# Six of the eight output-projection columns by seven-product blocks in a fused decoder layer

## The chip, the cores and the metric

The kernel runs on one NeuronCore of a Trainium2 chip. The metric is the device time of one execution in microseconds (us). Three timed runs of the kernel before gave 1549.17, 1547.85 and 1546.90 us; their median is 1547.85 us. Engines are named TensorE (PE; its weight loads are PEld), VectorE (DVE), ScalarE (ACT), GpSimd (POOL) and SyncE (SP, which issues most transfers).

## The reference

One layer of a decoder trunk, batch 1, 512 tokens, width 1024, all in float32:

```python
h = x + 0.5 * swiglu(rmsnorm(h, ffn1_norm), ffn1_w_in, ffn1_w_out)
h = h + hybrid_mixer(rmsnorm(h, mix_norm), ...)
h = h + 0.5 * swiglu(rmsnorm(h, ffn2_norm), ffn2_w_in, ffn2_w_out)
return rmsnorm(h, final_norm)

# the end of hybrid_mixer: two branches, merged by gates, then the output projection
y = sigmoid(gate_h) * y_h + sigmoid(gate_g) * y_g      # 512 x 1024
return y @ w_out                                       # w_out is 1024 x 1024
```

The change is in this last product `y @ w_out`, in what surrounds it (the merge ahead, the residual and the norm behind) and in the first steps of the second feed-forward block (FFN2).

## The kernel before

Activations lie transposed: a column tile is 128 features (partitions) by 512 tokens, so the width of 1024 is eight column tiles. A float32 product is made of three matmuls (`mm3`, lines 199 to 202): each operand is split into a high part, rounded by ScalarE, and a low part, the rest, subtracted by VectorE; high by high, high by low and low by high are summed in PSUM. So every slab of weights (128 x 512) costs a load, a ScalarE cast and a VectorE subtraction before TensorE can use it. The split weights lie in a ring of six buffers (`pair`, `WB = 6`), so a slab can be split once TensorE has finished the one six before it.

**Output projection** (lines 2250 to 2255). For each of eight columns d: the residual `hr` is loaded from `hd` in DRAM, `dense` does 8 blocks of 128 features with two slabs of four (24 matmuls of 512 tokens), VectorE adds half the sum to the residual (`h[:, d]`, line 2254), and `nextnorm` prepares FFN2: `prep` (line 224) writes `uh[:, d]` by ScalarE and `ul[:, d]` by VectorE, `sqacc` (line 230) squares the column on ScalarE and adds it to `acc`; here the add is GpSimd's, but for the first column (none) and the last (VectorE, line 697). The operands `ms[k]` come from `merged(k)` (lines 1900 to 1934): after the branch product of column k is complete, VectorE joins the gated branches, ScalarE and VectorE split the result.

**FFN2** (`ffn`, line 477; `stream`, line 292) runs units of four feature blocks in a fixed order: units 0 to 11 are plain (12 matmuls of 512 tokens, three pairs of columns p = 0, 1, 2), and from unit 12 on each pair is made of seven products of half the tokens (12 matmuls of 256; `seven`, `four`, `fast`): a 2 x 2 block of weights times a 2 x 2 block of activations by seven multiplications in place of eight, with sums of operands before and of results behind. `operands` (line 456) makes the activations' combinations. The norm of FFN2 comes late: units 0 to 3 run on values that are not divided by the root of the mean square yet. `stats` gives two steps, `sums` (eight narrow matmuls on `acc`, then VectorE and GpSimd for the root) and `spread` (the roots to all partitions, copied to `rbc` by ScalarE); they are hooked ahead of units 1 and 2 (line 530), and everything that needs `rbc` starts at unit 3 (`start = 3`).

**What sets the order.** The mixer up to `D.run()` and all of FFN2 have an order written out by the program (inside `manual_schedule`); for the mixer a planner (`Desk`) with costs per instruction and ranks hands out the engines' turns. The output projection between them is ordered by the framework's scheduler, which fills each engine's queue by its own estimate of when things are ready; the slab splits are marked `high_priority`. On the chip each queue then runs strictly in that order.

Of the kernel before, what the change touches and what calls it, by code (L numbers as in the profile page):

```python
# [29 lines left out]
C_F1, C_MX, C_F2, C_FN, C_HN, C_GN, C_LB, C_CV = 0, 8, 16, 24, 32, 33, 34, 50  # L30
# [15 lines left out]
TA = 6  # L46
# [102 lines left out]
def body(tc, xT, cst, sqc, hmask, dta, w1o, w1a, w2a, wt, wn, wab, wbh, wbg, wo, w1b, w2b, gfin, y, dbg=None):  # L149
# [91 lines left out]
    def stats(pl, *parts):  # L241

        def sums():
            pt = psc.tile([P, T], F32, tag="pd", name="pst")
            for i in range(NT):
                for n, x in enumerate(parts):
                    pe.matmul(pt[:, i:i + 1], x[:, i * P:(i + 1) * P], ones[:, :1], start=n == 0, stop=n == len(parts) - 1)
            root(pl, pt[:, :4], rcol)

        def spread():  # L250
            pb = psc.tile([P, T], F32, tag="pd", name="pbc")
            for i in range(NT):
# [224 lines left out]
    def ffn(w1, w2, c0, after, slow, lead=None, last=None):  # L477

        with tc.tile_pool(name="ff", bufs=1) as fp, \
# [40 lines left out]
            if lead is not None:  # L520
                pts, rest = opening(fp)
                lead()
                hooks[0] = [rest]
                for p in range(2):
                    f = columns([lambda x=x: x for x in pts[2 * p:2 * p + 2]], p, p == 1)
                    for t, x in zip((0, 0, 0, 1), f):
                        hooks.setdefault(t, []).append(x)
                done, start = 2, 1
            else:
                hooks[1], hooks[2] = ([f] for f in stats(fp, acc))  # L530
                start = 3
            for p in range(done, slow):
                us = []
                for n in range(2):
                    x, held = plain(w1[ORDER[p], n], KD, ux, lane("a" if lead is None else "b") if p == done and (lead is None or n == 0) else mm, fold=FOLD1[lead is None][p], roomy=lambda k: n if lead is not None or p else 0)
                    units += x
                    us.append((len(units) - 1, held))
                f = columns([lambda x=x: x["pt"] for _, x in us], p)
                on(max(us[0][0], start), f[0])
                on(us[1][0], f[1])  # L540
                on(us[1][0], f[2])
                hooks.setdefault(us[1][0] + 1, []).append(f[3])
            xo = operands(c0, xs, rooms, start, hooks)
            for p in range(slow, KF):
                units += fast(w1, p, xo, fp, len(units), posts, gate, late)
# [423 lines left out]
def mixer(tc, mp, e):  # L969
# [8 lines left out]
    def ps(name, lane="d"):  # L978
        return psc.tile([P, T], F32, tag="p" + lane, name=name, bufs=LANES[lane])
# [914 lines left out]
    def one(tag):  # L1894
# [2 lines left out]
            return ab[:, 0], ab[:, 1]  # L1897
        return make

    def merged(d):  # L1900

        yield "on", ("K", 7) if d < 2 else "projected", ("y", d), ("t", d), ("t", 8 + d), *([("ms", d - 3)] if d > 2 else [])
        yield "get", "mi", 1
        mi, tg = places["kn"]("mi"), places["vb"]("mt")
        yield S
        sp.dma_start(mi, md[d])
        yield S
        sp.dma_start(tg, td[d])
        g = stay.get(8 + d)
        if g is None:  # L1910
            yield "get", "ta", 1
            g = ta("mg")
            yield S
            sp.dma_start(g, td[8 + d])
        yield "lag", LAG["back"]
        yield V(512)
        dve.scalar_tensor_tensor(mi, tg, 1.0, mi, op0=ALU.add, op1=ALU.mult)
        yield "on", ("wbg", d)
        yield *V(512), 1
        dve.scalar_tensor_tensor(g, g, 1.0, pts[d], op0=ALU.add, op1=ALU.mult)  # L1920
        D.put("a" if d in (2, 3) else "mm")
        yield V(512)
        dve.tensor_tensor(g, g, mi, op=ALU.add)
        D.put("mi")
        if dbg is not None and "m" in dbg:
            sp.dma_start(dbg["m"][:, d], g)
        yield A(512)
        ab = op[d]("m", (P, 2, T), F32R)
        a, b = ms[d] = ab[:, 0], ab[:, 1]
        act.copy(a, g)  # L1930
        yield V(512)
        dve.tensor_tensor(b, g, a.bitcast(F32), op=ALU.subtract)
        D.put("ta")
        D.fire(("ms", d))

    def closing():

# [17 lines left out]

    o_h = [None] * HH
    so, ms, pts = [None] * VH, [None] * 8, {}
    stay = dict.fromkeys(STAY)
    wbgs = [(d, q) for q in range(3) for d in (0, 1)] + [(d, q) for d in (2, 3) for q in range(3)] + [(d, 3) for d in range(4)] + \
        [(d, q) for d in range(4, 8) for q in range(4)]  # L1960
    G = {"kq": [hv[:, i].rearrange("p (c a b) -> p c a b", c=NT, a=2) for i in range(3)]}
# [285 lines left out]
            sp.dma_start(dbg["og"][:, i], od[i])  # L2247


    for d in range(8):  # L2250
        hr = ta("hr")
        sp.dma_start(hr, hd[d])
        pt = dense(wo[d], KD, lambda k: ms[k])
        dve.scalar_tensor_tensor(h[:, d], pt, 0.5, hr, op0=ALU.mult, op1=ALU.add)
        e["nextnorm"](C_F2, tag="ta", bufs=TA)(d, mp)

# [80 lines left out]
```

## Time and profile before

| what | value |
|---|---|
| median of three runs | 1547.85 us |
| profiled execution, its own time | 1547.87 us |
| its span, first to last instruction | 1546.1 us |
| PE busy | 99% of the span |
| VectorE / ScalarE / GpSimd busy | 76% / 57% / 26% |
| share of PE in the chain that ended last | 96% |
| granted TensorE clock | 0.999 of full speed |

The span is read from the profile's first line; 1.8 us of the execution's time lie outside it. A busy PE says only that matmuls follow one another: whether one kind of matmul is cheaper than another is read from the distance of their starts. Idle time of an engine that is not the bottleneck costs nothing, but an average share hides stages in which another engine is nearly full, so busy times are read stage by stage.

### The profile page before, as it was taken

What the parts mean: (1) busy time and instruction counts of PE and PEld (TensorE: products, weight loads), DVE (VectorE), ACT (ScalarE), POOL (GpSimd) and SP (SyncE); (2) the same over time, 40 slices, a digit from 0 to 9 for tenths busy, and PEclk for the clock granted to TensorE, in tenths of its full rate; (3) what the DMA queues carried; (4) which work ended last, traced back from release to release, by engine and by line L of the source; (5) the groups of instructions that cost most, each with busy time, mean ns of one, the idle gap of its engine ahead of it and who ended that gap; (6) DMA issues with size and microseconds to landing.
All of it is one profiled execution on the core that took longest, in us unless ns stands there. A gap on an engine that the chain in (4) does not pass through costs nothing.

```text
span 1546.1 us, 29433 instructions
## 1 busy us (share of the span) xinstructions
PE 1535.9 (99%) x10660; PEld 1340.0 (87%) x10660; DVE 1179.7 (76%) x2257; ACT 887.9 (57%) x1965; POOL 409.0 (26%) x727
## 2 busy tenths in 40 slices
PE   9999999999999999999999999999999999999998
PEld 8899998988888888888888878888888899999897
DVE  6988887678786778678888887865554799988765
ACT  5766776454454345556676676555423576676543
POOL 0211221110221212536534655450001221121000
PEclk9999999999999999999999999999999999999999
DMA  5866866543213223654463675566554587786751
GB/s 190 190 167 171 190 163 150 154 120 109 84 45 94 65 81 117 191 181 147 134 208 119 190 224 164 171 191 187 153 192 130 157 185 194 194 194 172 192 123 64
DMA packets 159538, 237.57 MB, mean 154 GB/s; under 512 B 23312, under 2 KB 54672, under 8 KB 159392
## 3 DMA queue, kind: packets, MB, share of 16 engines
q1 hardware_dynamic: 138944, 199.63, 41.5%
q0 software_dynamic: 17568, 31.47, 12.7%
q10 hardware_dynamic: 2880, 4.59, 1.0%
q8 instruction: 84, 1.38, 0.4%
q14 instruction: 62, 0.51, 0.1%
HBM read 206.50 MB, written 29.13 MB: 152 GB/s over the span
## 4 chain that ended last, share of the span: by engine, by line
PE 96%; DMA 1%; ACT 1%; DVE 1%; issue 0%; SPq 0%; POOLq 0%; POOL 0%; ACTq 0%; DVEq 0%
PE pmm L200 17%; PE pmm L202 17%; PE pmm L201 17%; PE px L202 8%; PE px L200 8%; PE px L201 8%; PE pnat L200 4%; PE pnat L202 4%; PE pnat L201 4%; DMA kt<-kn 1%; PE pog L1738 1%; PE pgq L1530 1%; PE pw L1722 1%; PE pl L1277 1%; PE pd L1220 1%; PE pog L1736 1%
## 5 line engine op out<-in xcount | busy, mean ns | idle before, releaser
L200 PE MATMUL pmm<-uh,wp 128*128 128x512 f32 x863 | 355.2, 412 | 0.5 <-ACT ci L1397 0.3
L202 PE MATMUL pmm<-uh,wp 128*128 128x512 f32 x863 | 337.5, 391 | 0.0
L201 PE MATMUL pmm<-ul,wp 128*128 128x512 f32 x863 | 336.9, 390 | 0.0
L202 PE MATMUL px<-xs,wp 128*128 128x256 f32 x900 | 248.4, 276 | 0.0
L200 PE MATMUL px<-xs,wp 128*128 128x256 f32 x900 | 248.4, 276 | 0.0
L201 PE MATMUL px<-xs,wp 128*128 128x256 f32 x900 | 248.4, 276 | 0.0
L2103 DVE TENSOR_TENSOR wp<-raw,wp 128x512 fp32r<-128x512 f32 x226 | 159.3, 711 | 86.7 <-ACT wp L2101 83.5
L2101 ACT CAST wp<-raw 128x512 fp32r<-128x512 f32 x226 | 139.3, 619 | 137.0 <-PE pmm L202 106.5
L202 PEld LDWEIGHTS pmm<-uh,wp 128*128 128x128 f32 x863 | 162.0, 188 | 35.4
L200 PEld LDWEIGHTS pmm<-uh,wp 128*128 128x128 f32 x863 | 162.3, 188 | 33.2 <-ACT ci L1397 0.7
L201 PEld LDWEIGHTS pmm<-ul,wp 128*128 128x128 f32 x863 | 162.5, 188 | 29.7 <-DVE ul L1802 0.4
L200 PEld LDWEIGHTS px<-xs,wp 128*128 128x128 f32 x900 | 169.0, 188 | 0.1
L201 PEld LDWEIGHTS px<-xs,wp 128*128 128x128 f32 x900 | 168.9, 188 | 0.1
L202 PEld LDWEIGHTS px<-xs,wp 128*128 128x128 f32 x900 | 168.9, 188 | 0.0
L344 ACT CAST wp<-sw 128x512 fp32r<-128x512 f32 x176 | 107.9, 614 | 69.0 <-PE px L202 20.9
L319 DVE TENSOR_TENSOR wp<-sw,wp 128x512 fp32r<-128x512 f32 x176 | 120.8, 686 | 32.6 <-ACT wp L344 32.5
L344 ACT CAST wp<-rw 128x512 fp32r<-128x512 f32 (+1 forms) x132 | 80.7, 613 | 29.1 <-PE pnat L202 10.5
L1581 POOL TENSOR_TENSOR fm<-gfs,gln 128x60 f32<-128x60 f32 (+24 forms) x155 | 61.7, 398 | 92.8 <-DMA od<-zo 26.6
L1407 DVE SCALAR_TENSOR_TENSOR cy<-ci,cs,cy 128x512 f32<-128x512 f32 x96 | 72.2, 753 | 1.4
L1582 POOL TENSOR_TENSOR gln<-gln,fm 128x60 f32<-128x60 f32 (+24 forms) x155 | 64.4, 415 | 12.1
L349 POOL DMA_DIRECT2D wp<-w1b x40 | 34.7, 866 | 112.0 <-ACT wp L348 56.1
L378 DVE TENSOR_TENSOR sw<-rw 128x512 f32<-128x512 f32 x88 | 60.4, 686 | 1.7 <-DMA rw<-w2a 1.7
(587 smaller groups left out, 3496.4 us busy)
## 6 DMA issues: line engine op xcount, KB each, us to landing
raw<-wt SPq DMA_DIRECT2D x160, 256.0 KB
rw<-w1b SPq DMA_DIRECT2D x80, 256.0 KB
rw<-w1a SPq DMA_DIRECT2D x74, 256.0 KB
wp<-w1b POOLq DMA_DIRECT2D x40, 256.0 KB, 5.4
wp<-w1a POOLq DMA_DIRECT2D x35, 256.0 KB, 5.3
rw<-w2b SPq DMA_DIRECT2D x34, 256.0 KB
raw<-wn SPq DMA_DIRECT2D x32, 256.0 KB
raw<-wbg SPq DMA_DIRECT2D x32, 256.0 KB
```

The source lines that it names most:

```text
L200: pe.matmul(pt, ah, bh, start=first, stop=False)
L201: pe.matmul(pt, ah, bl, start=False, stop=False)
L202: pe.matmul(pt, al, bh, start=False, stop=last)
L319: dve.tensor_tensor(lo, x, hi.bitcast(F32), op=ALU.subtract)
L344: act.copy(hi, x)
L349: pool.dma_start(lo, units[i].fold, accum_op=ALU.add)
L378: dve.tensor_tensor(v[n], a, b, op=op)
L1407: dve.scalar_tensor_tensor(y, ci[:, j:j + T], wc[j], y, op0=ALU.mult, op1=ALU.add)
L1581: pool.tensor_tensor(tv, bc(m[:, j + 1:, j], w), t[:, j:j + 1, :w].to_broadcast([P, n, w]), op=ALU.mult)
L1582: pool.tensor_tensor(t[:, j + 1:, :w], t[:, j + 1:, :w], tv, op=ALU.add)
L2101: act.copy(hi, raw)
L2103: dve.tensor_tensor(lo, raw, hi.bitcast(F32), op=ALU.subtract)
```

## The change

Columns 0 and 1 stay as they were. Columns 2 and 3, 4 and 5, 6 and 7 are computed in pairs by `sevens(j)`, j = 1, 2, 3: seven products of 12 matmuls of 256 tokens each. `pieces(j)`, j = 0 to 3, makes the activations' combinations from the merged columns j and 4 + j, in place in `h` (where `merged` now leaves its result), and splits them; j = 0 to 2 run inside `merged(4)` to `merged(6)`, j = 3 ahead of the output projection. The residual of columns 2 to 5 is added by a transfer from `hd` that accumulates into `h`, issued by GpSimd; columns 6 and 7 load it as before and VectorE adds it. The squares of columns 1 to 6 are added to `acc` by VectorE. In FFN2 `sums`, `spread` and what needs `rbc` move back by one unit. `merged` also gives back its `ta` buffer earlier. The diff, cut where it repeats names:

```diff
+OUT = 0, 1, (2, 3), (4, 5), (6, 7)
...
-                hooks[1], hooks[2] = ([f] for f in stats(fp, acc))
-                start = 3
+                hooks[2], hooks[3] = ([f] for f in stats(fp, acc))
+                start = 4
...
-                on(us[1][0], f[1])
-                on(us[1][0], f[2])
-                hooks.setdefault(us[1][0] + 1, []).append(f[3])
+                t = max(us[1][0], start)
+                on(t, f[1])
+                on(t, f[2])
+                hooks.setdefault(t + 1, []).append(f[3])
...
+    def pieces(j):
+        x, y, lo, hi = h[:, j], h[:, 4 + j], slice(0, 256), slice(256, 512)
...
+        crossed[j] = homes[:2], homes[2:]
+        less = lambda o, a, b: (V(256), lambda: dve.tensor_tensor(o, a, b, op=ALU.subtract))
+        yield less(x[:, lo], x[:, hi], x[:, lo])
+        yield less(x[:, hi], y[:, hi], x[:, hi])
+        yield less(y[:, hi], y[:, hi], x[:, lo])
+        yield less(y[:, lo], y[:, lo], y[:, hi])
+        for z, (a, b) in zip((x, y), crossed[j]):
+            yield A(512), lambda z=z, a=a: act.copy(a, z)
+            yield V(512), lambda z=z, a=a, b=b: dve.tensor_tensor(b, z, a.bitcast(F32), op=ALU.subtract)
+
+    def sevens(j):
...
+        a11, a21, a22, a12 = (fetch(*x) for x in ((0, 0), (1, 0), (1, 1), (0, 1)))
+        bank = [ps("px", x) for x in "abde"]
+        where = {3: (0, lo), 5: (0, hi), 6: (1, lo), 0: (2, lo), 2: (2, hi), 1: (3, lo), 4: (3, hi)}
...
+        def comb(x, y, f):
+            z = places["kn"]("ws")
+            with tc.high_priority():
+                dve.tensor_tensor(z, x, y, op=f)
+            return z
+
+        def product(o, x):
+            wl, wh = e["pair"](off=SHIFT)
+            with tc.high_priority():
+                act.copy(wh, x)
+                dve.tensor_tensor(wl, x, wh.bitcast(F32), op=ALU.subtract)
+            b, c = where[o]
+            for i in range(4):
+                k, (m, t) = slice(i * P, i * P + P), moving[o](i)
+                mm3(bank[b][:, c], wh[:, k], wl[:, k], m[0][:, t], m[1][:, t], i == 0, i == 3)
+        product(0, a11)
+        s1 = comb(a21, a22, ALU.add)
+        s2 = comb(s1, a11, ALU.subtract)
+        product(2, s2)
...
+        act.mul(w[:, :256], bank[2][:, lo], 0.5)
+        dve.scalar_tensor_tensor(u, bank[2][:, hi], 0.5, w[:, :256], op0=ALU.mult, op1=ALU.add)
+        product(3, a12)
+        product(1, s1)
+        product(4, comb(a11, a21, ALU.subtract))
...
+        dve.scalar_tensor_tensor(uu, b4, 0.5, u4.to_broadcast([P, 2, 256]), op0=ALU.mult, op1=ALU.add)
+        dve.scalar_tensor_tensor(w[:, 768:], bank[3][:, lo], 0.5, w[:, 512:768], op0=ALU.mult, op1=ALU.add)
+        if j == 3:
+            for n in range(2):
+                hr = ta("hr")
+                sp.dma_start(hr, hd[2 * j + n])
+                x = w[:, n * T:n * T + T]
+                dve.tensor_tensor(x, hr, x, op=ALU.add)
+        product(6, a22)
+        product(5, comb(a12, s2, ALU.subtract))
+        act.copy(h[:, 2 * j + 1, hi], w[:, 768:])
+        for n, c in ((1, lo), (0, slice(0, T))):
+            dve.scalar_tensor_tensor(h[:, 2 * j + n, c], bank[n][:, c], 0.5, w[:, n * T:n * T + c.stop], op0=ALU.mult, op1=ALU.add)
+            if j < 3:
+                pool.dma_start(h[:, 2 * j + n], hd[2 * j + n], accum_op=ALU.add)
+        return 2 * j, 2 * j + 1
...
+        if 4 <= d < 7:
+            for need, f in pieces(d - 4):
+                yield need
+                f()
...
-    for d in range(8):
+    for need, f in pieces(3):
+        f()
+    after = e["nextnorm"](C_F2, tag="ta", bufs=TA, add=dve)
+    for step in OUT:
+        if isinstance(step, tuple):
+            for d in sevens(step[0] // 2):
+                after(d, mp)
+            continue
         hr = ta("hr")
-        sp.dma_start(hr, hd[d])
-        pt = dense(wo[d], KD, lambda k: ms[k])
-        dve.scalar_tensor_tensor(h[:, d], pt, 0.5, hr, op0=ALU.mult, op1=ALU.add)
-        e["nextnorm"](C_F2, tag="ta", bufs=TA)(d, mp)
+        sp.dma_start(hr, hd[step])
+        pt = dense(wo[step], KD, lambda k: ms[k])
+        dve.scalar_tensor_tensor(h[:, step], pt, 0.5, hr, op0=ALU.mult, op1=ALU.add)
+        after(step, mp)
```

## Rows read from the trace of the kernel before

**Rows 1.** The page's head: busy us, share of the span, instructions of each engine.
```profile
span 1546.1 us, 29433 instructions
PE 1535.9 (99%) x10660; PEld 1340.0 (87%) x10660; DVE 1179.7 (76%) x2257; ACT 887.9 (57%) x1965; POOL 409.0 (26%) x727
```

**Rows 2.** Stages: end of merge, output projection, FFN2's plain units, its seven-product units.
```profile
core 0: us, PE busy (x) PEld busy (x) DVE busy (x) ACT busy (x) POOL busy (x), PEclk, DMA share, GB/s
1144.50:1165.38 20.88, 20.88 (x94) 17.27 (x93) 8.83 (x14) 5.60 (x9) 0.00 (x0) 1.00 0.30 93
1165.38:1208.90 43.52, 43.52 (x194) 36.05 (x193) 21.78 (x32) 18.28 (x30) 7.87 (x6) 1.00 0.41 128
...
1217.20:1243.64 26.44, 26.44 (x119) 21.86 (x118) 24.77 (x31) 18.56 (x27) 6.09 (x7) 1.00 0.75 171
1243.64:1291.20 47.56, 47.56 (x421) 47.56 (x420) 44.27 (x71) 34.11 (x63) 11.23 (x13) 1.00 0.83 200
```

**Rows 3.** TensorE's timeline: start us, us, what (idle before, releaser).
```profile
1165.38 0.39 PE L200 MATMUL pmm<-m,wp 128*128 128x512 f32 x1
...
1208.90 0.39 PE L200 MATMUL pmm<-uh,wp 128*128 128x512 f32 x1
...
1246.37 0.28 PE L200 MATMUL px<-xs,ws 128*128 128x256 f32 x1
...
1247.73 0.28 PE L200 MATMUL px<-xs,wp 128*128 128x256 f32 x1
...
1251.81 0.28 PE L200 MATMUL px<-xs,wp 128*128 128x256 f32 x1
```

**Rows 4.** Weight loads by line in 1243.64:1291.20: busy us, mean ns, idle before.
```profile
L201 PEld LDWEIGHTS px<-xs,wp 128*128 128x128 f32 x124 | 23.3, 188 | 0.0
```

**Rows 5.** VectorE's timeline in FFN2 where it hardly rests.
```profile
1260.17 0.69 DVE L436 TENSOR_TENSOR luu<-px,lv 128x512 f32<-128x512 f32 x1 [0.34 <-PE px L202]
1260.90 0.42 DVE L437 TENSOR_TENSOR lv<-px,luu 128x256 f32<-128x256 f32 x1
1261.24 0.69 DVE L319 TENSOR_TENSOR wp<-sw,wp 128x512 fp32r<-128x512 f32 x1
1261.84 0.69 DVE L378 TENSOR_TENSOR sw<-rw 128x512 f32<-128x512 f32 x1
```

**Rows 6.** VectorE's timeline around the first columns of the output projection.
```profile
1163.56 0.69 DVE L196 TENSOR_TENSOR wp<-raw,wp 128x512 fp32r<-128x512 f32 x1 [2.03 <-ACT wp L195]
1165.58 0.69 DVE L1920 SCALAR_TENSOR_TENSOR tg<-tg,pmm 128x512 f32<-128x512 f32 x1 [1.33 <-PE pmm L202]
1168.26 0.69 DVE L1932 TENSOR_TENSOR m<-tg,m 128x512 fp32r<-128x512 f32 x1 [0.69 <-ACT m L1930]
1175.77 0.75 DVE L227 SCALAR_TENSOR_TENSOR ul<-h,cs,uh 128x512 fp32r<-128x512 f32 x1
1176.46 0.69 DVE L2254 SCALAR_TENSOR_TENSOR h<-pmm,hr 128x512 f32<-128x512 f32 x1
```

**Rows 7.** Transfers by issuing line, from the page: KB each, median us to landing.
```profile
wp<-w1b POOLq DMA_DIRECT2D x40, 256.0 KB, 5.4
```

**Rows 8.** ScalarE's timeline at the end of the output projection.
```profile
1210.72 0.71 ACT L226 ACTIVATE uh<-h,cs 128x512 fp32r<-128x512 f32 x1
```

**Rows 9.** VectorE's timeline from the projection's end into FFN2, and its next idle times.
```profile
1209.10 0.69 DVE L2254 SCALAR_TENSOR_TENSOR h<-pmm,hr 128x512 f32<-128x512 f32 x1 [2.67 <-PE pmm L202]
...
1211.61 0.75 DVE L227 SCALAR_TENSOR_TENSOR ul<-h,cs,uh 128x512 fp32r<-128x512 f32 x1
...
1217.22 2.74 DVE L467 SCALAR_TENSOR_TENSOR rooma<-h,cs,rbc 128x512 f32<-128x512 f32 x4
...
1222.08 0.69 DVE L516 TENSOR_TENSOR lv<-pmm,rbc 128x512 f32<-128x512 f32 x1 [1.51 <-PE pmm L202]
...
1248.61 0.68 DVE L319 TENSOR_TENSOR wp<-sw,wp 128x512 fp32r<-128x512 f32 x1
1250.65 0.69 DVE L436 TENSOR_TENSOR luu<-px,lv 128x512 f32<-128x512 f32 x1 [1.36 <-PE px L202]
```

More of the change, by code (lines that the diff above doesn't have):

```diff
@@ L1898, in one @@
         return make
+    def pieces(j):
+        x, y, lo, hi = h[:, j], h[:, 4 + j], slice(0, 256), slice(256, 512)
+        if j == 0:
+            homes = [t[:, i] for t in (places["gz"]("wz", (P, 2, T), F32R) for _ in range(2)) for i in range(2)]
+        elif j < 3:
+            homes = [places[n]("wq", dt=F32R) for n in (("on", "on", "qm", "ln"), ("gb", "gb", "at", "at"))[j - 1]]
+        else:
+            homes = [z[:, 6 + i] for i in range(2) for z in (uh, ul)]
+        crossed[j] = homes[:2], homes[2:]
[7 more added lines that the diff above has]
+            yield V(512), lambda z=z, a=a, b=b: dve.tensor_tensor(b, z, a.bitcast(F32), op=ALU.subtract)
@@ new lines, in sevens, with fetch @@
+    def sevens(j):
+        def fetch(n, q):
+            r = places["vb"]("wr")
+            sp.dma_start(r, wo[2 * j + n][:, q * T:q * T + T])
+            return r
+        lo, hi = slice(0, 256), slice(256, 512)
+        moving = {0: lambda i: (ms[i], lo), 3: lambda i: (ms[4 + i], lo), 5: lambda i: (ms[4 + i], hi),
+                  1: lambda i: (crossed[i][0], lo), 4: lambda i: (crossed[i][0], hi),
+                  6: lambda i: (crossed[i][1], lo), 2: lambda i: (crossed[i][1], hi)}
+        a11, a21, a22, a12 = (fetch(*x) for x in ((0, 0), (1, 0), (1, 1), (0, 1)))
[19 more added lines that the diff above has]
+        product(2, s2)
+        w = places["n2"]("wv", (P, 4 * 256))
+        u = places["x"]("wu", (P, 256))
+        act.mul(w[:, :256], bank[2][:, lo], 0.5)
[3 more added lines that the diff above has]
+        product(4, comb(a11, a21, ALU.subtract))
+        uu, b4, u4 = (y.rearrange("p (a t) -> p a t", t=256) for y in (w[:, 256:768], bank[3], u))
+        dve.scalar_tensor_tensor(uu, b4, 0.5, u4.to_broadcast([P, 2, 256]), op0=ALU.mult, op1=ALU.add)
[14 more added lines that the diff above has]
+        return 2 * j, 2 * j + 1
@@ L1919, in merged @@
         yield *V(512), 1
-        dve.scalar_tensor_tensor(g, g, 1.0, pts[d], op0=ALU.add, op1=ALU.mult)
+        gt = g
+        dve.scalar_tensor_tensor(gt, gt, 1.0, pts[d], op0=ALU.add, op1=ALU.mult)
         D.put("a" if d in (2, 3) else "mm")
         yield V(512)
-        dve.tensor_tensor(g, g, mi, op=ALU.add)
+        g = h[:, d]
+        dve.tensor_tensor(g, gt, mi, op=ALU.add)
         D.put("mi")
+        D.put("ta")
         if dbg is not None and "m" in dbg:
@@ L1932, in merged @@
         dve.tensor_tensor(b, g, a.bitcast(F32), op=ALU.subtract)
-        D.put("ta")
         D.fire(("ms", d))
+        if 4 <= d < 7:
+            for need, f in pieces(d - 4):
+                yield need
+                f()
     def closing():
@@ L1957, in mixer @@
     so, ms, pts = [None] * VH, [None] * 8, {}
-    stay = dict.fromkeys(STAY)
+    stay, crossed = dict.fromkeys(STAY), {}
     wbgs = [(d, q) for q in range(3) for d in (0, 1)] + [(d, q) for d in (2, 3) for q in range(3)] + [(d, 3) for d in range(4)] + \
```

## The prediction

> **What bounds the kernel now.** I read the page's head first: TensorE is busy for 99% of the span, VectorE for 76% [rows 1]. An average hides stages, so the second view is busy time by stage [rows 2]: TensorE has no hole in any of them; VectorE works half of the output projection's time (21.78 of 43.52 us), but 24.77 of 26.44 us in FFN2's plain units and 44.27 of 47.56 us in its seven-product units. The reader is to see two things there: the projection is paced by TensorE alone, and VectorE is nearly as full in the stage right behind. The third view is TensorE's timeline, since a busy matmul says nothing of its price. The projection's 192 matmuls of 512 tokens start at 1165.38 and FFN2's first at 1208.90, so 43.52 / 192 = 0.2267 us each; one product of 12 matmuls of 256 tokens goes from 1246.37 to 1247.73, so 0.1133 us each [rows 3]. Half the tokens cost exactly half the time.
>
> **What TensorE saves.** Removed: 6 columns x 24 x 0.2267 = 32.64 us. Added: 3 pairs x 7 products x 12 x 0.1133 = 28.56 us. The saving is an eighth, **4.08 us**; the projection would take 39.44 us (10.88 for columns 0 and 1, 9.52 per pair). No change of `pieces` or of the transfers can add to that, so 1547.85 - 4.08 = 1543.8 us is the floor.
>
> Here a rule speaks against the change. The row: a weight load is listed at 188 ns [rows 4], longer than the 113 ns of the matmul that it serves, and loads cover all 47.56 us of the seven-product stage against 36.05 of 43.52 us in the projection [rows 2]. The Trainium skill, "Perfetto Trace Analysis" (Identifying the Most-Contended Engine), says that TensorE's headroom is to be judged by the share of time in weight loads rather than by matmul busy time; by that rule the new form has none and the old one has 17%. The starts in rows 3 decide against reading it as a price: loads run beneath matmuls, and 256 tokens still cost half of 512.
>
> **What VectorE must do instead.** Instructions that follow one another closely start 0.60 us apart for 512 elements (1261.24 to 1261.84), 0.34 for 256 (1260.90 to 1261.24), 0.73 where the next needs the result (1260.17 to 1260.90) [rows 5], and 0.69 for `ul` (1175.77 to 1176.46) [rows 6].
>
> - One pair, what TensorE waits for: 7 low parts x 0.60 = 4.2; 4 sums of weights x 0.60 and 0.13 for the one that needs its predecessor = 2.5; results out of PSUM 3 x 0.34 + 0.73 + 0.60 = 2.35. Together **9.1 us** beside 9.52 us of TensorE.
> - One pair, what follows: two `ul` and two additions to `acc`, 2 x (0.69 + 0.60) = **2.6 us**. So 11.7 us of VectorE per 9.52 us of TensorE: VectorE becomes the fuller engine, by 2.2 us a pair. The additions were GpSimd's (7.87 us over the stage [rows 2], off every path), so that move brings nothing on TensorE's side and costs VectorE 6 x 0.60.
> - Before the pairs, from 1165.38 on: the rest of `merged(7)`, 3 x 0.63 = 1.9; `pieces(3)`, 4 x 0.34 + 2 x 0.60 = 2.6; columns 0 and 1 with `ul` and one addition, 3.2.
> - The residual of columns 6 and 7, 1.2. Low parts of FFN2's first two slabs, 1.2.
>
> `pieces(0)` to `pieces(2)`, 2.6 us each, fall into the merge, where VectorE is busy 8.83 of 20.88 us [rows 2]: hidden; without that cover they would add to the same queue, up to 7.8 us. The first product's low part and two sums also run ahead there (1.9 us): slabs are split as soon as the ring of six frees a place, which is why VectorE waits 2.03 us for ScalarE's cast at 1163.56 [rows 6]. `pieces(3)` can start once column 7 is merged (1168.95, the end of the L1932 row in rows 6) and is first needed in the second product of the first pair, at 1165.38 + 10.88 + 1.36 = 1177.6: hidden. ScalarE gains 7 casts a pair and some copies beside 18.28 of 43.52 us [rows 2]: hidden as long as nothing blocks its queue. A pair's weights come by four loads of 256 KB on SP as before; GpSimd's queue holds only the four accumulating issues.
>
> Sum of VectorE's work from 1165.38 to the last `ul`: 1.9 + 2.6 + 3.2 + 3 x 11.7 + 1.2 + 1.2 - 1.9 = **43.3 us**. TensorE needs `ul` of column 7 at the eighth feature block of FFN2: 39.44 + 7 x 3 x 0.2267 = **44.2 us**. So the plan holds only if VectorE rests less than 0.9 us in 44, and it cannot:
>
> - In the first 10.88 us the ring lets it split only four products; there are 1.9 + 2.6 + 2.4 + 1.2 (two sums) + 1.3 = 9.4 us of work: 1.5 us idle.
> - The residual of columns 2 to 5 comes by accumulating transfers; the same kind lands 5.4 us after its issue [rows 7]. The follow-up of a pair can't start before, so 2.6 us of it move into the next pair's last third. The second pair's results leave at about 30.8 us, its data land at about 36.5 us, and its 2.6 us crowd into the end. I take 1.0 us of idling; below it could be nothing (other splits fill in), above see the second rival.
> - Behind the last product: its matmul needs 0.28 us to end, then 0.34 + 0.60 us of results, then ScalarE's `uh` of 0.71 us [rows 8], before the `ul` of columns 6 and 7 can go. Before, that tail took from 1209.10 to 1212.36 [rows 9]. I take 1.1 us that nothing else fills.
>
> 43.3 + 3.6 = 46.9 us against 44.2: TensorE waits **2.7 us** in FFN2's first two units, with ends at 0.6 (only the first idling) and, if the transfers block the queues, about 8. `acc` is complete some 0.6 us behind; `sums` now stands one unit later, 5.44 us behind FFN2's start, and is covered by the same wait.
>
> **FFN2, one unit later.** `rbc` is ready 2.72 us later than before, and with it VectorE's long run of work, which started at 1217.22 and was worked off at 1249.3 [rows 9]. In that run VectorE waited 1.51 us for TensorE at 1222.08, which now is filled; 1.2 us remain. The low part that ended at 1249.29 was used by the matmul of 1251.81 [rows 3, 9], 2.5 us later, so 1.2 us are covered: cost 0. If that cover is gone, up to 1.2 us.
>
> **Sum.** -4.08 + 2.7 = -1.4 us. In the profiled execution (span 1546.1, own time 1547.87 us, 0.02 above the median of the runs) the span would be 1544.7; from the median, **1546.5 us**. About 0.2%, 3.1 us, is what a measurement of this kernel tells from no change, so faster means under 1544.75 and slower over 1550.95. The forecast is no change that can be told.
>
> **Rivals.**
>
> 1. *No wait appears* (29%): VectorE's necessary part is 9.1 of 9.52 us per pair, FFN2's seven-product units do well with it at 93% [rows 2], and low parts may overtake the follow-up work, which has some units' time. Then 1543.8 to 1544.7 us. Against it: the `ul` have a due time, 44.2 us, and 43.3 us of work in front.
> 2. *The queues block on the transfers* (23%): the order of the projection's queues is fixed before the run. If `uh` and `sq` of columns 2 to 5 are queued as if their data landed in half of 5.4 us [rows 7], ScalarE and VectorE stand still 2.7 us twice, with the next pair's casts, low parts and sums behind them, and VectorE has no rest to make it up: TensorE waits 2.7 + 5.4 = 8.1 us, 1547.85 - 4.08 + 8.1 = **1551.9 us, slower**. It ends above the time before from 0.7 us of blocking per pair, and above 1550.95 from 2.25 us. For it: VectorE's lack of rest; against it: a ring of six splits gives about 8 us of lead at the start.
> 3. *The later norm costs* (2%): 1.2 us in FFN2, 1547.7 us.
> 4. *Weight loads pace the products* (1%): 252 x 0.188 = 47.4 us against 32.6, 1562.6 us; rows 3 speak against it. That is the skill's rule above taken as a price.
>
> The change not doing its work, the planner's turns in the merge going another way, would be a wait of VectorE on a buffer among 1144 and 1165; 12 us of rest there [rows 2] make me give it nothing apart.
>
> **The numbers.** The forecast has 45%; its own range, from 1.4 us to 4.7 us of waiting, is 1545.2 to 1548.5. Rival 1 is all faster: 0.29. Of rival 2's 0.23 some 0.02 (blocking under 2.25 us) stays within: slower 0.21 and rival 4's 0.01, so 0.22. The rest is the same: 0.49. The range for 8 in 10 runs from just above the floor, 1544.0, to rival 2's time, 1551.9.
>
> **What would show it.** The projection's products 1.36 us apart, first to last 39.4 us: the saving is right. Idle time of TensorE ahead of FFN2's first matmuls or before `pst`, released by VectorE's `ul`, a low part (L319) or `acc`: the forecast's wait, 2.7 us in sum; none: rival 1. ScalarE's `uh` of columns 2 to 5 with idle time ended by a transfer, over 1 us each: rival 2. VectorE's busy share over 90% from 1176 to 1215: the ledger is right; under 80%, it is wrong. TensorE idle between units 12 and 20 of FFN2: rival 3. Matmuls of 256 tokens over 0.12 us apart would make the whole sum wrong.

## The result, and the profile after

The changed kernel takes **1557.36 us** (median of four runs, 1555.00 to 1558.39) beside 1547.91 us for the kernel before in the same comparison: a ratio of 1.0056, 95% interval 1.0043 to 1.0068. It is slower by 9.4 us where no change was forecast, and outside the range. The profiled execution took 1557.5 us.

The page's head of the kernel after says as little as that of before [rows 1]: TensorE is "99% busy".

```profile
span 1555.7 us, 29723 instructions
PE 1538.8 (99%) x10768; PEld 1345.6 (86%) x10768; DVE 1210.1 (78%) x2319; ACT 897.8 (58%) x1988; POOL 401.4 (26%) x725
```

Busy time by stage of the kernel after, to be laid beside [rows 2]; the column behind POOL is the granted clock: end of the merge, projection, the stretch that the forecast named, the first units of FFN2, the same up to VectorE's last `ul`, and two stretches at the lower clock.

```profile
core 0: us, PE busy (x) PEld busy (x) DVE busy (x) ACT busy (x) POOL busy (x), PEclk, DMA share, GB/s
1144.50:1166.91 22.41, 22.41 (x100) 18.55 (x99) 16.35 (x29) 8.40 (x14) 0.00 (x0) 1.00 0.34 109
1166.91:1211.28 44.37, 42.37 (x303) 39.88 (x302) 36.64 (x64) 23.78 (x44) 3.55 (x4) 0.96 0.35 90
1176.00:1215.00 39.00, 37.00 (x278) 35.15 (x276) 33.94 (x59) 20.40 (x38) 3.55 (x4) 0.96 0.39 97
1211.28:1228.40 17.12, 13.42 (x52) 10.14 (x51) 10.16 (x19) 7.31 (x13) 1.45 (x2) 0.80 0.50 161
...
1211.28:1220.77 9.49, 5.85 (x22) 3.60 (x20) 8.79 (x16) 4.31 (x8) 0.00 (x0) 0.93 0.19 55
...
1202.40:1205.81 3.41, 3.41 (x19) 3.41 (x18) 3.41 (x7) 0.48 (x2) 1.72 (x2) 0.50 0.21 36
1219.47:1226.30 6.83, 6.30 (x19) 4.99 (x19) 2.67 (x5) 1.19 (x3) 0.41 (x1) 0.50 0.69 217
```

The projection takes 44.4 us instead of the 39.4 that the sum gave (two matmuls of FFN2, 0.45 us, run inside it), and FFN2's first units now contain holes. Where they are, TensorE's timeline shows (start, duration, idle before and its releaser in brackets):

```profile
1200.27 0.38 PE L201 MATMUL px<-m,wp 128*128 128x256 f32 x1 [1.87 <-ACT wp L1943]
...
1202.77 0.41 PE L201 MATMUL px<-wz,wp 128*128 128x256 f32 x1
1202.98 0.41 PE L202 MATMUL px<-wz,wp 128*128 128x256 f32 x1
...
1217.92 0.50 PE L201 MATMUL pmm<-uh,wp 128*128 128x512 f32 x1 [2.82 <-ACT uh L227]
1218.77 0.50 PE L202 MATMUL pmm<-ul,wp 128*128 128x512 f32 x1 [0.35 <-DVE ul L228]
1220.83 0.80 PE L202 MATMUL pmm<-ul,wp 128*128 128x512 f32 x1 [0.46 <-DVE ul L228]
1221.85 1.70 PE L248 MATMUL pst<-ones,acc 128*128 128x1 f32 x8
```

Two kinds of loss are to be seen. One is the waits. The other follows the two long ones (1.87 and 2.82 us): from 1202.40 the matmuls of 256 tokens start 0.213 us apart instead of 0.113, because the granted clock is 0.50 (1.2 instead of 2.4 GHz). The kernel before has no such stretch here.

**The sum from the trace.** From the projection's first matmul to FFN2's unit 12 the kernel before takes 78.26 us (1165.38 to 1243.64), the kernel after 86.10 (1166.91 to 1253.01): +7.84. The distances between starts give the terms: -4.08 saved; +0.5 of small delays between matmuls; +4.3 in the projection (2.8 of waiting, 1.5 at half clock); +7.1 from 1214.7 to 1228 (some 5 of waiting, 2 at half clock). Behind unit 12 both kernels take the same time (302.47 and 302.72). Of the profiled run's other 1.8 us, 1.53 lie ahead of the projection: its start varies between 1165.05 and 1167.01 over the traces of this study, with the work ahead unchanged in all kernels but the one before.

**Why it waits: ScalarE's queue.** Its timeline in the kernel after:

```profile
1190.52 0.62 ACT L1943 CAST wp<-wr 128x512 fp32r<-128x512 f32 x1
...
1195.74 0.72 ACT L227 ACTIVATE uh<-h,cs 128x512 fp32r<-128x512 f32 x1 [4.32 <-DMA h<-hd]
1197.95 0.72 ACT L227 ACTIVATE uh<-h,cs 128x512 fp32r<-128x512 f32 x1 [1.48 <-DMA h<-hd]
1198.58 1.14 ACT L237 ACTIVATE sqt<-h 128x512 f32<-128x512 f32 x2
1199.62 0.60 ACT L1943 CAST wp<-wr 128x512 fp32r<-128x512 f32 x1
...
1207.31 0.72 ACT L227 ACTIVATE uh<-h,cs 128x512 fp32r<-128x512 f32 x1 [0.85 <-DMA h<-hd]
...
1216.11 1.14 ACT L345 CAST wp<-raw 128x512 fp32r<-128x512 f32 x2 [0.44 <-DMA raw<-w1b]
1217.15 0.72 ACT L227 ACTIVATE uh<-h,cs 128x512 fp32r<-128x512 f32 x1
```

`uh` of columns 2 and 3 stands still until the accumulating transfers land, and the cast that TensorE needs at 1200.27 is queued behind it. The last cast ahead of this block ended at 1191.14, the next began at 1199.62; TensorE ran dry at 1198.40, 7.3 us into the gap of 8.5. GpSimd issued the transfers at 1189.32; the four of this kind landed after 4.2 to 8.0 us, in the median 5.4 as in [rows 7]. The last two rows belong to the other long wait, that of 2.82 us: `uh` of column 6 stands behind two casts of FFN2's slabs.

**Why it waits: VectorE's tail.** Its timeline in the kernel after, which answers to [rows 9]:

```profile
1195.92 0.69 DVE L1937 TENSOR_TENSOR ws<-wr 128x512 f32<-128x512 f32 x1 [3.65 <-DMA wr<-wo]
...
1212.14 0.69 DVE L1968 TENSOR_TENSOR wv<-hr,wv 128x512 f32<-128x512 f32 x1
1212.74 0.69 DVE L320 TENSOR_TENSOR wp<-raw,wp 128x512 fp32r<-128x512 f32 x1
...
1215.14 1.02 DVE L1973 SCALAR_TENSOR_TENSOR h<-px,wv 128x512 f32<-128x512 f32 x2
1216.76 1.29 DVE L320 TENSOR_TENSOR wp<-raw,wp 128x512 fp32r<-128x512 f32 x2 [0.59 <-ACT wp L345]
1217.97 0.74 DVE L228 SCALAR_TENSOR_TENSOR ul<-h,cs,uh 128x512 fp32r<-128x512 f32 x1
...
1220.03 0.75 DVE L228 SCALAR_TENSOR_TENSOR ul<-h,cs,uh 128x512 fp32r<-128x512 f32 x1
```

The last product runs from 1209.44 to 1211.45, but its results leave PSUM at 1215.14: VectorE is 3.7 us behind, and low parts of FFN2's slabs (L320) and the residual of columns 6 and 7 (L1968) stand in front. The last `ul` ends at 1220.8; the projection was over at 1211.3.

### The profile page after: what moved, and what is told of

It is laid out like the page before. It is cut to its first block, busy times and chain, and to the rows that moved or that the text cites. A ratio compares the mean times of both kernels' runs of the same rounds, so it can differ in the third digit from the quotient of the medians.

```text
span 1555.7 us, 29723 instructions
## 1 busy us (share of the span) xinstructions
PE 1538.8 (99%) x10768; PEld 1345.6 (86%) x10768; DVE 1210.1 (78%) x2319; ACT 897.8 (58%) x1988; POOL 401.4 (26%) x725
## 4 chain that ended last, share of the span: by engine, by line
PE 91%; DMA 3%; DVE 2%; ACT 1%; issue 1%; SPq 1%; POOLq 0%; ACTq 0%; POOL 0%; DVEq 0%
PE pmm L201 16%; PE pmm L203 15%; PE pmm L202 15%; PE px L202 8%; PE px L203 8%; PE px L201 8%; PE pnat L201 4%; PE pnat L203 4%; PE pnat L202 4%; DMA kt<-kn 2%; PE pog L1740 1%; PE pgq L1532 1%; PE pw L1724 1%; PE pl L1279 1%; PE pd L1222 1%
## 5 line engine op out<-in xcount | busy, mean ns | idle before, releaser
L320 DVE TENSOR_TENSOR wp<-sw,wp 128x512 fp32r<-128x512 f32 x176 | 120.6, 685 | 32.9 <-ACT wp L345 32.8
```

Of the source, the lines that this page charges most:

```text
L320: dve.tensor_tensor(lo, x, hi.bitcast(F32), op=ALU.subtract)
```

## The experiments

"To unit 12" is the stretch of the sum above, in one profiled execution of each, and "half clock" is the time at 1.2 GHz within it. All runs stand beside runs of the kernel before on their chip (medians 1547.7 to 1548.1 us). The intervals are 3 to 5 us wide, so a difference of under about 2 us between two runs is read from the traces and not from the medians.

| run | edit | us | ratio, 95% | to unit 12 | half clock, us |
|---|---|---|---|---|---|
| - | before | 1547.9 | 1 | 78.26 | none |
| - | after | 1557.36 | 1.0056 (1.0043-1.0068) | 86.10 | 10.2 |
| 1 | no residual for columns 2-5 | 1552.67 | 1.0033 (1.0020-1.0046) | 83.06 | 10.2 |
| 2 | weights of 4, 5 in other buffers | 1557.40 | 1.0059 (1.0043-1.0076) | 87.81 | 13.7 |
| 3 | all residuals loaded | 1554.29 | 1.0041 (1.0026-1.0056) | 84.09 | 10.2 |
| 4 | 2 and 3 | 1554.49 | 1.0040 (1.0025-1.0055) | 83.06 | 10.2 |
| 5 | 1, squares on GpSimd | 1552.66 | 1.0033 (1.0020-1.0046) | 82.95 | 6.8 |
| 6 | 1, filler matmuls | 1553.36 | 1.0034 (1.0022-1.0046) | 83.70 | 3.4 |
| 7 | 3, nine low parts folded | 1553.67 | 1.0038 (1.0023-1.0053) | 83.34 | 6.8 |
| 8 | pairs only for 4-7 | 1556.35 | 1.0054 (1.0037-1.0071) | 85.65 | 6.8 |
| 9 | 4, tail's order | 1552.78 | 1.0033 (1.0020-1.0045) | 82.42 | 10.2 |
| 10 | 9, FFN2's units in turns | 1550.84 | 1.0021 (1.0011-1.0030) | 80.78 | 6.8 |
| 11 | 10, norm later again | 1555.01 | 1.0045 (1.0030-1.0060) | 78.75 | 3.4 |
| 12 | 11, squares on GpSimd | 1556.72 | 1.0052 (1.0037-1.0067) | 81.07 | 6.8 |
| 13 | 10, fewer early casts | 1552.97 | 1.0031 (1.0019-1.0043) | 81.65 | 6.8 |
| 14 | 13, norm later again | 1557.17 | 1.0060 (1.0045-1.0075) | 86.10 | 13.7 |
| 15 | 13, no residual for 2-5 | 1550.39 | 1.0018 (1.0009-1.0028) | 79.28 | 3.4 |
| 16 | pairs only for 2-5, in the middle | **1546.47** | 0.9991 (0.9981-1.0000) | 76.39 | none |
| 17 | 16, squares on GpSimd | 1551.30 | 1.0022 (1.0012-1.0031) | 80.07 | 3.4 |
| 18 | 16, norm one unit later | 1546.92 | 0.9996 (0.9986-1.0005) | 77.07 | none |

### The transfers (runs 1 to 4)

Run 1:

```diff
-            if j < 3:
-                pool.dma_start(h[:, 2 * j + n], hd[2 * j + n], accum_op=ALU.add)
```

> The changed kernel, but the residual of columns 2 to 5 is left out altogether (no accumulating transfer; the output lacks that term). Theory 'blocked queues' (ScalarE stands 4.3 + 1.5 us on the first residual, TensorE then waits and its clock falls to half): the waits on h<-hd go, the tail behind the projection shortens, some 4 to 7 us less than the changed kernel, 1550 to 1553 us; the 3.7 us that VectorE stands on weights (wr<-wo) stay. Theory 'too much work on VectorE': the work taken out is none of VectorE's, so 1556 to 1558 us.

Without the accumulating transfers the median is 4.7 us lower, of which the trace shows 3.0 up to unit 12: ScalarE's waits for `h<-hd` are gone and the projection is over in 41.0 us. The other 5.0 us over the kernel before remain, as waits of TensorE for `uh` and `ul` in FFN2's first units, with 10.2 us at half clock.

Run 2, the weights of columns 4 and 5 in other buffers than the ring of four:

```diff
-            r = places["vb"]("wr")
+            r = places["vb" if j != 2 else ("t64", "at")[q]]("wr")
```

> The changed kernel, but the weights of columns 4 and 5 are loaded into four other buffers, so that those of columns 6 and 7 need not wait for theirs. Theory 'blocked queues' with the weights as the cause: VectorE's 3.7 us on wr<-wo go, 2 to 4 us less, 1553 to 1555 us; with the residual transfer as the cause ScalarE still stands 4 us in the same place: within 1 us of the changed kernel, 1556 to 1558. Theory 'too much work on VectorE': 1556 to 1558 us too.

The projection shortens to 40.5 us and nothing is won: the wait stands in FFN2 instead (5.18 us at 1217.18). ScalarE still stands for `h<-hd`, 2.95, 0.49, 1.70 and 3.62 us, and yet TensorE has no hole in the projection. So the late weights (VectorE's 3.65 us at 1195.92) had a part in the hole there, but were no cause of the loss by themselves.

Runs 3 and 4, the residual of all pairs by SP's loads and VectorE (`if j == 3:` becomes `if True:`), without and with the other buffers:

> The changed kernel, but the residual of all six columns is loaded beforehand and added by VectorE, as it is for columns 6 and 7; no accumulating transfer. VectorE gets 4 more additions, 2.4 us. Theory 'blocked queues' (residual): no ScalarE wait on h<-hd, 2 to 5 us less than the changed kernel, 1552 to 1555 us. Theory 'too much work on VectorE': 2.4 us more, 1559 to 1561 us.

> Both: four other buffers for the weights of columns 4 and 5, and the residual of all six columns loaded and added by VectorE. Theory 'blocked queues' (either): neither engine waits for data in the projection, TensorE keeps its full clock there, what stays is the tail of my forecast with 2.4 us of more additions: 1547 to 1550 us. Theory 'too much work on VectorE': 1559 to 1561 us.

Taking the residual off the transfers is worth 3.1 us in run 3, 1.6 less than leaving it out, at the price of four more additions on VectorE. In run 4 the projection is free of waits (40.0 us), yet the time is the same: the loss is now behind it, 3.79 us of waiting at 1213.29 and 10.2 us at half clock.

### Taking work off VectorE, and filling TensorE (runs 5 to 8)

Run 5, the squares on GpSimd as before the change:

```diff
-    after = e["nextnorm"](C_F2, tag="ta", bufs=TA, add=dve)
+    after = e["nextnorm"](C_F2, tag="ta", bufs=TA)
```

> The changed kernel without the residual of columns 2 to 5 (left out, as in the run e1_nores, 1552.67 us) and with the squares of columns 1 to 6 added by GpSimd as before the change. Theory 'VectorE's work sets the tail': 6 additions of 0.60 us less, so the 5.4 us that TensorE waits behind the projection shrink by 2 to 3.6 us and less time at half clock: 1547 to 1550.5 us. Theory 'the order at the end of the queues sets the tail, not the amount': within 1 us of 1552.7.

No gain, though six additions of 0.6 us are off VectorE. Run 17 shows why.

Run 6, `fill(20)` behind the projection: 20 matmuls whose result is not used.

> As e1_nores (residual of columns 2 to 5 left out), with 20 matmuls of 512 tokens into an unused PSUM bank put between the projection and FFN2, 4.5 us of TensorE, so that its wait there is spent busy. Theory 'the fall to half clock costs by itself': the clock stays at full speed, the 2.6 us and more that FFN2's first units and the norm's matmuls lose at half clock come back: 1549 to 1550.5 us. Theory 'only the wait costs, the slow matmuls hide in it': 1552 to 1554 us.

TensorE then waits 2.81 us for the root ahead of `pbc`, and the clock falls there. Keeping the engine busy moves the wait down the same chain, acc to root to `rbc`.

Run 7, the low parts of products 0, 3 and 6 as in FFN2: ScalarE writes minus the high part, a transfer adds the weights.

```diff
+                if o in FOLDS:
+                    act.mul(wl, wh.bitcast(F32), -1.0)
+                    pool.dma_start(wl, src[id(x)], accum_op=ALU.add)
...
```

> As e3_load (residual of all six columns added by VectorE, 1554.29 us), with the low parts of the three products per pair that take raw weights made by ScalarE (minus the high part) and an accumulating transfer of the weights, as FFN2 does, in place of VectorE's subtraction: 9 x 0.60 = 5.4 us less of VectorE. Theory 'VectorE's work sets the tail': 1547.5 to 1550.5 us. Theory 'order at the end of the queues': 1553 to 1556 us. If the low parts land too late for their product, TensorE waits in the projection: over 1556.

5.4 us less on VectorE bring 0.6, which the medians can't tell from nothing; the transfers land late, and TensorE waits 1.30 and 1.40 us for them inside the projection.

Run 8, `OUT = 0, 1, 2, 3, (4, 5), (6, 7)`:

> The changed kernel with columns 2 and 3 computed as before, so four columns by seven products instead of six. By my ledger VectorE has 3.5 us less to do and TensorE 1.4 us more, so the tail shrinks by up to 4.9 us; one residual transfer (columns 4 and 5) still stands in the queues. Theory 'VectorE's work': 1551 to 1554 us. Theory 'order and blocked queues alone': 1556 to 1558 us.

Two pairs at the end cost nearly as much as three. But the transfers of columns 4 and 5 stand right ahead of the last pair, and VectorE's timeline in run 8 shows it waiting for `uh`, which ScalarE writes only once they have landed:

```profile
1202.58 0.75 DVE L228 SCALAR_TENSOR_TENSOR ul<-h,cs,uh 128x512 fp32r<-128x512 f32 x1 [2.28 <-ACT uh L227]
...
1204.85 0.75 DVE L228 SCALAR_TENSOR_TENSOR ul<-h,cs,uh 128x512 fp32r<-128x512 f32 x1 [1.18 <-ACT uh L227]
```

So run 8 doesn't tell the place of the pairs from the transfers.

### Order and due time (runs 9 to 15)

Run 9, on run 4: FFN2's fifth and sixth slab are cast only after unit 2, and the tail's instructions have high priority.

```diff
+            if hold < 0 or t > 1:
-            ahead(t, 2)
+                ahead(t, 2)
...
+        with tc.high_priority():
+            act.copy(h[:, 2 * j + 1, hi], w[:, 768:])
...
```

> As the run with all residuals loaded and the weights of columns 4 and 5 in other buffers (1554.5 us), but FFN2's fifth and sixth slab are split only after unit 2's steps, and the residual adds, results, uh and ul of the pairs are marked high priority. If the order at the end of the queues is what is late, VectorE's last ul comes 1.5 to 2 us earlier (two low parts of 0.6 us and the 0.5 to 1 us of waiting for a raw slab are gone from in front of it): 1552 to 1553 us. If VectorE's amount of work alone sets it, 1554 to 1555 us. If the half clock comes by any wait, it is still there (over 3 us at 0.5).

0.6 us less than run 4 in the stretch to unit 12 (1.7 in the median): this order counts for little.

Run 10: the first four units read columns 0 to 3 twice before columns 4 to 7, so `uh` and `ul` of the late columns come due 2.7 us later.

```diff
+                if lead is None and p == done:
+                    units[1], units[2] = units[2], units[1]
...
```

> As the run before it, and FFN2's first four units in the order first half of column a, first half of column b, second half of a, second half of b: uh and ul of columns 4 to 7 come due 5.4 to 7.5 us behind the projection's end instead of 2.7 to 4.8. If the due time of these is what makes TensorE wait, the waits in units 0 and 1 go; the sums of the norm still stand ahead of unit 2 and wait for acc, about 2 to 3 us: 1549 to 1552 us. If the wait only moves to the sums in full, 1552 to 1553 us.

1.9 us better in the median, 1.6 in the stretch. No wait for `uh` or `ul` is left; one of 4.2 us for `acc` ahead of the sums is. VectorE's busy time in run 10, in the projection and up to its last `ul`:

```profile
1165.43:1205.30 39.87, 39.87 (x303) 37.89 (x302) 37.20 (x66) 23.20 (x42) 0.00 (x0) 1.00 0.20 63
...
1165.43:1215.40 49.97, 45.76 (x328) 42.55 (x327) 46.02 (x80) 28.44 (x51) 0.00 (x0) 0.97 0.23 71
```

The projection has no hole at all, VectorE works 93% of it, and still has nearly 9 us to do. ScalarE's share of the tail, in run 10:

```profile
1210.49 1.14 ACT L345 CAST wp<-raw 128x512 fp32r<-128x512 f32 x2 [3.66 <-DMA raw<-w1b]
1211.53 0.40 ACT L1976 COPY h<-wv 128x256 f32<-128x256 f32 x1
1211.84 0.72 ACT L227 ACTIVATE uh<-h,cs 128x512 fp32r<-128x512 f32 x1
```

Runs 11 and 12, the norm's sums and spread at units 3 and 4, and the same with GpSimd's squares:

> As the run before it, and the sums, the spread and what needs them one more unit later (units 3 and 4, start at 5). If the cause is due times alone, nothing waits for more than 1 us any more, TensorE's clock stays at full speed and the saving of 4.08 us shows: 1544.5 to 1547 us, faster than the kernel before. If the later norm costs VectorE's run in the seven-product units, 1.2 to 2.7 us of new idle time shows there: 1547 to 1549 us. If the late acc follows whatever the order, 1551 to 1553 us.

> As the run before it, with the squares of columns 1 to 6 added by GpSimd again, 3.6 us less on VectorE. If VectorE's amount of work still decides, 1 to 2 us faster than the run before it: 1544 to 1546 us. If GpSimd's adds lengthen VectorE's instructions beside them, as seen in an earlier run (1.7 to 2.4 us instead of 0.7), or acc comes later by them, no gain or slower: 1546 to 1549 us.

Up to unit 12 run 11 is nearly at the kernel before (78.75), and then it loses 6 us: TensorE waits 3.19 us for a folded slab at 1251.99, which my edit of the look-ahead had made late at least in part: run 14, where it is restored, loses 2.4 us there. So run 11 is no clean answer. Run 12 takes 2.3 us more than run 11 up to unit 12; its executions (1553.47 to 1556.97 us) overlap with those of run 11 (1553.53 to 1555.71). The 2.4 us that its expectation names is a row of two instructions; single ones took up to 1.79 us in run 5.

Run 13 was to take the casts at 1210.49 out of the tail, run 14 to repeat run 11 with the look-ahead restored, run 15 is run 13 without the residual of columns 2 to 5.

> As the run with FFN2's first four units in turns (1550.8 us, where ScalarE stood 3.66 us at the cast of FFN2's fourth slab, ahead of uh of columns 6 and 7), but that cast is issued only behind them. If the order of ScalarE's queue is what is late, uh and ul of column 6 come 1 us earlier, acc and the sums 1 to 1.5 us earlier, and 1549 to 1550 us come out. If VectorE's amount of work sets the tail (46.0 us of work in the 50.0 us up to its last ul), no change: 1550.5 to 1551 us.

> As the run before it, and the sums, the spread and what needs them one unit later, now without the loss of lead of FFN2's slabs that the earlier run with late sums had (its 3.19 us of waiting for a folded slab at 1251.99). If due times decide, no wait over 1 us is left ahead of unit 12 and 1545 to 1547.5 us come out. If the later norm itself costs, new idle time of 1 to 3 us between units 12 and 20: 1547.5 to 1550 us.

> As the first run of this call, with the residual of columns 2 to 5 left out (their result lacks it): 2.4 us less on VectorE with the same order of the queues. If VectorE's amount of work decides, 2 us faster than the first run: 1547 to 1548.5 us. If the order alone decides, under 0.7 us faster.

Run 13 missed its aim: two casts still stand there (at 1211.95, after 4.18 us of waiting for `raw<-w1b`), so whether that block costs by itself stays open; it is 2.1 us slower than run 10 in the median and 0.9 up to unit 12. Run 14 is slower again: a wait of 2.81 us for the root ahead of `pbc`, two of 0.93 and 0.75 us behind unit 12, 13.7 us at half clock.

Run 15 against run 13 tests VectorE's amount of work: four additions (2.4 us) less, 2.37 us less to unit 12 and 2.6 us in the median. The two agree in part by luck. From the projection's first matmul to VectorE's last `ul`, in run 13 and run 15:

```profile
core 0: us, PE busy (x) PEld busy (x) DVE busy (x) ACT busy (x) POOL busy (x), PEclk, DMA share, GB/s
1166.95:1216.85 49.90, 45.76 (x328) 42.55 (x327) 45.43 (x79) 28.34 (x51) 0.00 (x0) 0.99 0.23 72
...
1165.78:1214.92 49.14, 45.92 (x331) 42.67 (x329) 43.46 (x75) 28.24 (x51) 0.00 (x0) 1.00 0.17 52
```

VectorE works 2.0 us less and is done only 0.8 us earlier, because it rests more (1.16 us for a residual, `hr<-hd`). TensorE's wait for `acc` shrinks from 4.14 to 3.22 us; the rest of the 2.37 us goes with 3.4 us less at half clock. So less work helps, by less than its own length.

### Room for VectorE at the end (runs 16 to 18)

Run 16 has both edits of run 4, the sums back at units 1 and 2 (`start = 3`), and plain columns last:

```diff
-OUT = 0, 1, (2, 3), (4, 5), (6, 7)
+OUT = 0, 1, (2, 3), (4, 5), 6, 7
```

> Only columns 2 to 5 by seven products, columns 6 and 7 by 24 matmuls each behind them as before the change; all residuals loaded, sums and spread back at units 1 and 2. TensorE saves 2.72 us instead of 4.08. VectorE has 6.3 us of work in the last 10.88 us of the projection, and 4.6 us to work off what the two pairs left. If VectorE's lateness at the end of the projection is the cause, almost no wait is left in FFN2 and no half clock: 1545 to 1546.5 us, faster than the kernel before. If the pairs cost by themselves (transfers, weights, half clock inside the projection), 1548 us or more.

**1546.47 us**, 1.6 us under the kernel before at the edge of what can be told, and 10.9 under the kernel after. TensorE saves 2.72 us and gives back 0.9 (by the distance of starts; the timeline's bracket has 0.75), its only wait, at the sums. In run 16 VectorE is busy for 90% of the projection, nearly as full as in run 10 (93%), but done in time, and the clock stays whole:

```profile
1165.15:1205.80 40.65, 40.65 (x264) 36.90 (x263) 36.42 (x63) 23.84 (x42) 0.00 (x0) 1.00 0.27 89
1205.80:1211.00 5.20, 4.45 (x24) 3.55 (x23) 4.63 (x9) 2.39 (x4) 0.01 (x1) 1.00 0.04 7
```

Run 17, run 16 with the squares on GpSimd (the edit of run 5):

> As the run with two pairs and columns 6 and 7 by 24 matmuls (1546.5 us, one wait of 0.91 us for acc ahead of the sums), with the squares of columns 1 to 6 added by GpSimd as before the change: 3.0 us less on VectorE inside the projection. If VectorE's amount of work makes acc late, the 0.91 us goes: 1545.4 to 1546 us. If GpSimd's additions lengthen VectorE's instructions beside them or acc follows later, no gain or slower: 1546.3 to 1548 us.

4.8 us slower. `ul` by line (busy us, mean ns) and three rows of GpSimd's and VectorE's timelines in run 17; in run 16 the same line has 6.0 us and a mean of 745 ns:

```profile
L228 DVE SCALAR_TENSOR_TENSOR ul<-h,cs,uh 128x512 fp32r<-128x512 f32 x8 | 10.3, 1296 | 0.5 <-ACT uh L227 0.5
```

```profile
1191.38 3.08 POOL L239 TENSOR_TENSOR acc<-acc,sqt 128x512 f32<-128x512 f32 x2 [9.75 <-ACT sqt L237]
...
1191.85 3.15 DVE L228 SCALAR_TENSOR_TENSOR ul<-h,cs,uh 128x512 fp32r<-128x512 f32 x2
...
1207.24 1.77 DVE L228 SCALAR_TENSOR_TENSOR ul<-h,cs,uh 128x512 fp32r<-128x512 f32 x1
```

What VectorE is spared in additions (0.6 us each) it loses on the instruction beside them (1.77 against 0.75 us for one), `acc` is late by 2.8 us, and the clock falls after that wait.

Run 18, run 16 with the sums at units 2 and 3 (`start = 4`):

> As the run with two pairs, with the sums and the spread at units 2 and 3 as in the change. If the later norm costs nothing as the prediction had it, the wait of 0.91 us goes and 1545.4 to 1546 us come out. If it costs (up to 1.2 us of VectorE's cover, or a wait of 2.8 us for the root on GpSimd as in the run with late sums), 1546.5 to 1549 us, with new idle time of TensorE in units 3 to 20.

The medians of runs 16 and 18 can't be told apart; in the traces the wait at the sums goes and one of 1.39 us ahead of `pbc` comes. VectorE's timeline in run 18 shows the root (`rcol`) behind two low parts, which wait for a slab that ScalarE has not cast, while the sums (`pst`) started at 1211.65:

```profile
1214.37 0.69 DVE L320 TENSOR_TENSOR ws<-rw,ws 128x512 fp32r<-128x512 f32 x1 [3.69 <-ACT ws L345]
1214.98 0.69 DVE L320 TENSOR_TENSOR wp<-rw,wp 128x512 fp32r<-128x512 f32 x1
1215.58 0.16 DVE L262 TENSOR_SCALAR rcol<-pst 128x4 f32<-128x4 f32 x1
```

Run 18 differs from run 4 by a single edit, the last pair made plain, and takes 7.6 us less. This shows that the loss hangs on the last pair. It doesn't show whether the place or the number of the pairs decides: no run has two pairs at the end with both edits of run 4.

## Why the prediction was wrong

VectorE's busy time from the projection's first matmul to its last `ul`, to be laid beside the prediction's sum of work and rest: in the kernel after, in run 4 and in run 16.

```profile
core 0: us, PE busy (x) PEld busy (x) DVE busy (x) ACT busy (x) POOL busy (x), PEclk, DMA share, GB/s
1166.91:1220.78 53.87, 48.22 (x323) 43.48 (x321) 45.44 (x78) 28.09 (x51) 3.55 (x4) 0.96 0.32 84
...
1165.47:1216.13 50.66, 46.48 (x323) 41.82 (x321) 47.21 (x82) 28.77 (x51) 0.00 (x0) 0.96 0.22 72
...
1165.15:1210.27 45.12, 44.37 (x283) 39.77 (x281) 40.89 (x70) 26.23 (x46) 0.00 (x0) 1.00 0.24 81
```

- **The saving was right.** Products of 256 tokens start 0.113 us apart; run 10's projection takes 40.0 us without a wait, and 0.45 of it are two matmuls of FFN2 that run inside it, so the sum's 39.4 holds. Rival 4 is out.
- **"43.3 + 3.6 = 46.9 us against 44.2."** This step failed: VectorE's rest was mis-sized most, its work less. In the kernel after the work is 45.4 us and the rest 8.4, so the last `ul` is ready at 53.9 us, 9.7 behind its due time and not 2.7. Up to the matmul that uses it TensorE has lost those 9.7 of its 11.9 us (4.08 + 7.84). The work: the ledger counted two of FFN2's slabs; six low parts stand in front of the last `ul`, 2.4 us more. The rest: 3.65 us are a wait for late weights (`wr<-wo`), which the prediction put at nothing ("four loads of 256 KB on SP as before"), and 2.6 us lie in the first 11 us, where 1.5 were forecast. In run 4, where the weights have room and no residual comes by transfer, the rest is 3.5 us, about as forecast; its work is 47.2 us, with four residual additions more. The busy share from 1176 to 1215 is 87%, just under the 90% that I had set as proof.
- **"The residual of columns 2 to 5 ... I take 1.0 us of idling."** VectorE's own waits for the transfers were about that (0.22 and 0.89 us, on `uh`). What failed is that ScalarE's queue was left out of the sum, and rival 2 is what happened there: `uh` queued ahead of the next casts, ScalarE still for 4.32 and 1.48 us, then 0.85. With the late weights it cost 4.3 us inside the projection; without the transfers the projection is 3.3 us shorter (run 1). The argument against it, about 8 us of lead from the ring, was right in size (7.3 us until TensorE ran dry), but the block between two casts lasted 8.5 us.
- **"I take 1.1 us that nothing else fills" and "TensorE waits 2.7 us."** The second failed. TensorE's brackets behind the projection add up to 2.1 to 7.6 us in runs 1 to 10, whose last columns are a pair, with or without the transfers. In run 9, whose projection has no hole, the last `ul` ends 10 us behind the projection where 4.8 were due; 2.4 us of these are its four residual additions. Run 15 against 13 shows that the amount of work counts, by less than its length; runs 5 and 7 take work away and win nothing, because each puts another price in its place.
- **The clock was not in the sum.** Two stretches at 1.2 GHz, 10.2 us together, cost about 3.5 us by the distances of starts. A wait was priced at its length alone; here they cost nearly half as much again.
- **"That move brings nothing on TensorE's side" (the squares on VectorE).** Wrong where VectorE is full: in the form with two pairs the old place costs 4.8 us (run 17). With three pairs the medians show no gain of either (runs 1 and 5). In the kernel before `ul` keeps 0.75 us, since GpSimd's addition comes behind it, where VectorE mostly waits (one runs from 1178.51 for 1.34 us, VectorE rests 1.18 us up to 1179.88).
- **"FFN2, one unit later: cost 0."** Nearly right in time, incomplete in mechanism: no new wait behind unit 12 (rival 3), but 0.7 us more to unit 12 in run 18's trace than in run 16's, because the root falls behind slab work in VectorE's queue.

Rival 2 had 1551.9 us, for 5.4 us of blocking on top of the forecast's 2.7; the measured time is 5.5 us above it; the late weights, the larger work and the clock are what it lacked. What stays open: how much of the lateness behind the projection is the order of ScalarE's queue (run 13 did not change it), whether the place or the number of the pairs decides, and why the clock falls after some waits and not after others.

## What to carry to other kernels

When a change frees the busiest engine by loading the next one, add up that engine's work with its due time, including the following stage's early work that the scheduler puts in front; here a balance of 43.3 us of work against 44.2 was a loss, because the rest came to 8.4 us. Two pairs in the middle with plain work behind them is the form that lost nothing. Don't queue an instruction that waits for a transfer ahead of casts that feed the busiest engine. Price TensorE's waits with the stretch at half clock that may follow them.

## What the runs showed of the hardware

- The granted clock stayed at 1.00 after TensorE's waits of 0.75 us in run 16, 1.39 in run 18 and 1.30 and 1.40 in run 7's projection. It went to 0.50 (1.2 instead of 2.4 GHz) around or behind those of 1.87 and 2.82 us in the kernel after, 4.21 in run 10 and 2.82 in run 17, and in run 11 behind shorter ones close together (0.88 and 0.69 us, and two under 0.3 between them).
- Where four loads of weights, two of residual and two accumulating transfers of 256 KB each were under way in 17 us (1183 to 1200), the two accumulating ones landed after 7.2 us in the median, the later after 8.0; over all four of the projection the median is 5.4.
- GpSimd's additions of 512 elements (1.49 us each in run 17) stretched VectorE's two-input instructions beside them from 0.75 to 1.77 us. The Trainium skill, "GPSIMD Engine Reference" (Specifications), says that the two engines share their way to SBUF and contend where a VectorE instruction has two inputs there; the trace agrees, and gives the size.
